# An MoE layer's row gathers, emitted one block further ahead on GpSimd

## The chip, the cores and the metric

The kernel runs on one core of one Trainium2 chip. The metric is the time of one execution on the device, in microseconds. Each number for the whole kernel is the median of three runs.

## The reference

The reference is one decoder layer over 1024 tokens of width 1024, in float32: a mixer (attention heads and RWKV-7 heads), and behind it a mixture of experts. Only the second part is touched here. Each token goes to 6 of 64 experts, and every expert is a SwiGLU with an inner width of 256:

```python
def swiglu(x, wg, wu, wd):
    return (jax.nn.silu(x @ wg) * (x @ wu)) @ wd
...
    def block(args):
        tok, w, e = args
        y = swiglu(h[tok], w_gate[e], w_up[e], w_down[e])
        return y * w[:, None]
...
    x = x + g2 * moe_ffn(h, ...)
return rms_norm(x, final_g)
```

So for each block of assignments the rows of its tokens are gathered, multiplied with three matrices of one expert, weighted, and summed by token. A shared expert does the same for all tokens.

## The kernel before, in words

The mixer and the router take the first 1130 us or so. Then the MoE part runs over a list of blocks (`blocks`, lines 2038 to 2040). Blocks 0 to 7 are the shared expert on 128 tokens each. Blocks 8 to 91 are the routed ones: the experts are ranked by how many tokens they got, an expert has one to four blocks, and a block has 24 to 128 rows. 84 routed blocks belong to 64 experts. What doesn't fit into these blocks would be done in a loop at the end (`rest`).

For a routed block the work is this:

- **Slots** (`slots`, line 1932): an indirect DMA issued by GpSimd reads the list `sl` of the block from `d_slot`, a token number and a weight for each row.
- **Gather** (`rows`, line 1940): an indirect DMA issued by GpSimd reads the token rows from `d_h2` into `xg`, one of 4 buffers of 128 x 1024. The token numbers in `sl` are its indices, so it needs the slots landed.
- **Turn** (`turn`, lines 1952 and 1965): TensorE transposes the rows into `tp`; ScalarE and VectorE write a high and a low part, `xh` and `xl`. These are the transposes that need the gather landed.
- **Up** (`up`, line 1976), **SwiGLU** and **down** (`down`, line 1976 with output `yd`): matmuls in split precision with the parts of the weights.
- **Product** (`result`, line 2026): VectorE multiplies the two halves of `yd` by the row's weight and the gate `g2` into `ye`, one of 3 buffers.
- **Scatter** (`result`, line 2028): an indirect DMA issued by GpSimd adds `ye` to the rows of `d_acc`. All scatters write the same tensor, so each waits until the one before it has landed.

Each expert's weights, 3 MB, are loaded by SyncE (`fetch`, line 1884) a few experts ahead, and split into parts by ScalarE (`guh`, `wdh`) and VectorE (`gul` at line 1898, `wdl` at line 1905).

The order on each engine is the order in which the loop in `experts` emits, and an engine does its instructions in that order. In round `b` of the loop the up matmuls of block `b` are emitted, then the gather of block `b + 3` and the slots of block `b + 5`, then the turn of block `b + 1`, the down matmuls of block `b - 1` and last the product and the scatter of block `b - 1`:

```python
elif b > 6:
    need_x(b + 3)
if b > 7:
    need_s(b + 5)
...
if b > 0:
    result(zs, blocks[b - 1][2], weight_of(b - 1), tis[b - 1])
```

GpSimd thus has, for each round, a gather, a list of slots and a scatter. `need_t` emits no instruction: it takes the column of token numbers out of `sl`. The first five lists of slots are emitted by `dispatch` (line 2085), before the routed blocks. `final` (line 2198) loads `d_acc` once all scatters have landed, and takes the last norm.

Of the kernel before, what the change touches and what calls it, by code (L numbers as in the profile page):

```python
# [8 lines left out]
F32 = mybir.dt.float32  # L9
# [28 lines left out]
class Kern:  # L38
# [1804 lines left out]
    def phase_b(self, pg, close_a4, h2):  # L1843
# [6 lines left out]
        B, sets, wds, xts = {}, [], [], []  # L1850
# [22 lines left out]
        def expert_pools():  # L1873
            close_a4()
            B["wp"] = wp = pool("bw1", 1, side="right")
            sets.append(weight_set(wp))
# [51 lines left out]
            yield [("set", ("shared w", 0))]  # L1928

        def slots(idx, n):  # L1930
            sl = B["fp"].tile([128, 2], F32, name="sl", bufs=8)
            nc.gpsimd.indirect_dma_start(out=sl[0:n], out_offset=None, in_=self.d_slot, in_offset=ind(idx[0:n]))  # L1932
            return sl

        def tokens(sl, n):
            return sl.bitcast(I32)[0:n, 0:1]

        def rows(ti, n):
            x = B["fp"].tile([128, D], F32, name="xg", bufs=4)
            nc.gpsimd.indirect_dma_start(out=x[0:n], out_offset=None, in_=self.d_h2, in_offset=ind(ti), bounds_check=T - 1,  # L1940
                                         oob_is_err=False)
            return x
# [101 lines left out]
        def need_w(k):  # L2044

            for kk, to, which in ((k, raws, GU), (k - 1, rawd, DN)):
                if 0 < kk < NK:
                    to[kk] = fetch(self.eid[0:1, order[kk]:order[kk] + 1], which)

        def need_s(b):  # L2050
            if b < NB:
                k, j, n = blocks[b]
                r = order[k]
                sls[b] = slots(self.sidx[j][:, r:r + 1], n) if r >= 0 else None

        def need_t(b):
            if b < NB:
                tis[b] = tokens(sls[b], blocks[b][2]) if sls[b] else self.toki[:, b:b + 1]

        def need_x(b):  # L2060
            if b < NB:
                k, j, n = blocks[b]
                if k == 0:
                    x = xs[b] = B["fp"].tile([128, D], F32, name="xg", bufs=4)
                    nc.sync.dma_start(x, self.d_ht[j])
                else:
                    xs[b] = rows(tis[b], n)
# [4 lines left out]
        def pieces(n):  # L2072
            for _ in range(n):
                while work and next(work[0], "end") == "end":
                    work.pop(0)

        def dispatch():
            yield [("wait", ("route", 7))]
            expert_pools()
            yield from self.ranks(pg)  # L2080
            for k in range(1, 4):
                need_w(k)
            yield from self.leftover(pg)
            yield [("wait", ("block pools", 0))]
            for b in range(8, 13):
                need_s(b)
                yield [("POOL", 1.0)]
            yield [("DMA", 4.0)]
            yield [("set", ("slots", 0))]

        def experts():

            yield [("wait", ("block pools", 0))]
            yield [("wait", ("shared w", 0))]
            for b in range(8):
                i = blocks[b][1]
                sls[b], tis[b] = None, self.toki[:, i:i + 1]
            xs[0] = h2[6]
            for b in (1, 2):
                need_x(b)  # L2100
            G = ("alloc", ("g", 2)), ("free", "g")
            xt = turn(xs[0], 128)
            yield [("PE", .9), ("ACT", 1.0), ("~DVE", 1.2)]
            act = None
            for b in range(NB + 1):
                if b < NB:
                    k, j, n = blocks[b]
                    m = max(n, MIN_M)
                    two = xt[1] is None
                    for s in up(xt, sets[k % 2], m):  # L2110
                        if b < 8:
                            yield s
                    z = B["z"]
                    if b < 5:
                        yield [("wait", ("T", blocks[b + 3][1]))]
                        need_x(b + 3)
                    elif b == 6:
                        yield [("wait", ("slots", 0))]
                        for i in range(8, 12):
                            need_t(i)  # L2120
                        need_x(8)
                        need_x(9)
                    elif b > 6:
                        need_x(b + 3)
                    if b > 7:
                        need_s(b + 5)
                    turnover = k + 1 < NK + 1 and (blocks[b - 1][0] != k if k else b == 6)
                    if turnover and k + 1 < NK:
                        work.append(split_gu(raws[k + 1], k + 1))
                    pieces(3)  # L2130
                    if turnover and b < 8:
                        yield [("~ACT", 1.7), ("~DVE*", 1.8)]
                if b < NB and two:
                    low(z)
                if act is not None:
                    at = act_t(*act)
                    if b < 8:
                        yield [G[0], ("PE", .25), ("ACT", .3), ("DVE", .35), G[1]]
                if b + 1 < NB:
                    xt = turn(xs[b + 1], blocks[b + 1][2], b < 7)  # L2140
                    if b < 8:
                        yield [("~ACT", 1.0), ("~DVE*", 1.2)]
                if b < NB and two:
                    join(z)
                if act is not None:
                    for s in down(at, act[1]):
                        if b < 8:
                            yield s
                    zs = B["zs"]
                if b < NB:  # L2150
                    act = swiglu(z, m), m
                    pieces(99)
                    if b < 8:
                        yield [("~ACT", .6), ("~DVE", .35)]
                if b > 0:
                    result(zs, blocks[b - 1][2], weight_of(b - 1), tis[b - 1])
                    if b < 8:
                        yield [("~DVE", 1.35), ("~POOL", 1.0)]
                if b < NB:
                    if k and blocks[b - 1][0] != k:  # L2160
                        work.append(split_d(rawd[k]))
                        pieces(99)
                    if b > 7:
                        need_t(b + 4)
                    if turnover:
                        need_w(k + 4)
                    if turnover and b < 8:
                        yield [("~ACT", 2.0), ("~DVE", 2.3), ("~POOL", 1.0)]
# [93 lines left out]
```

## Time and profile before

| | us |
|---|---|
| median of 3 runs (lowest, highest) | 2097.12 (2080.12, 2115.2) |
| profiled execution | 2093.02 |
| its span, first to last instruction | 2091.1 |

| engine, whole span | busy us | share |
|---|---|---|
| TensorE (PE) | 1858.6 | 89% |
| VectorE (DVE) | 1470.3 | 70% |
| ScalarE (ACT) | 933.1 | 45% |
| GpSimd (POOL) | 859.6 | 41% |

A row of a timeline gives an instruction's start, its duration, the engine, the line, the operation and what it writes and reads; in brackets stands how long the engine was idle before it and what ended that. An indirect DMA on POOL is busy there while GpSimd issues it; its data lands later. "Issue" as the end of a wait means that the profile shows nothing that ended it.

### The profile page before, as it was taken

Reading aid. Unit: us, or ns where it says so; the run is one execution under the profiler, and the core shown is the slowest. Engines: PE = TensorE matmul, PEld = TensorE weight load, DVE = VectorE, ACT = ScalarE, POOL = GpSimd, SP = SyncE. Lnnn points to the kernel's source line nnn. Section 1 sums busy time; section 2 is a strip of 40 time slices with the busy share of each in tenths; the row PEclk is TensorE's granted clock in tenths of the full one; section 3 lists DMA queues with packets and bytes.
Section 4 is the critical chain, followed back from the end, with each engine's and each line's share of the span. In section 5 each row is a group of like instructions: output and inputs, shape, how many; then the busy total and the mean of one; then the engine's idle time right before and its main releaser. Section 6 shows DMA issues by size and latency. Waiting matters only on the chain. (4 is left out here: it accounts for less than half of the span.)

```text
span 2091.1 us, 28436 instructions
## 1 busy us (share of the span) xinstructions
PE 1858.6 (89%) x9729; PEld 1399.2 (67%) x9729; DVE 1470.3 (70%) x2561; ACT 933.1 (45%) x1431; POOL 859.6 (41%) x660
## 2 busy tenths in 40 slices
PE   3999999969997997997999799989988989989993
PEld 3777677747876664654787687767756767766771
DVE  7736867939457555656677758878767878878894
ACT  5443433312322332344323236556545656666673
POOL 1201110100012232335455634765656767766662
PEclk7999789969987888998999899999989999999997
DMA  7125345462756648964664589989889999988874
GB/s 270 36 81 126 88 111 129 131 156 71 216 148 183 190 123 237 133 195 137 229 211 147 159 277 322 314 256 318 293 261 309 304 305 307 326 297 297 307 242 174
DMA packets 268579, 440.03 MB, mean 210 GB/s; under 512 B 127445, under 2 KB 197161, under 8 KB 242450
## 3 DMA queue, kind: packets, MB, share of 16 engines
q1 hardware_dynamic: 210978, 365.47, 54.0%
q0 software_dynamic: 26176, 58.91, 12.4%
q10 hardware_dynamic: 31280, 13.83, 2.5%
q8 instruction: 78, 1.28, 0.3%
q14 instruction: 67, 0.55, 0.1%
HBM read 355.27 MB, written 94.90 MB: 215 GB/s over the span
## 5 line engine op out<-in xcount | busy, mean ns | idle before, releaser
L2028 POOL DMA_INDIRECT d_acc<-ye,sl x84 | 192.1, 2287 | 253.4 <-issue 56.2
L1932 POOL DMA_INDIRECT sl<-d_slot,d_sidx x84 | 201.6, 2400 | 27.5 <-issue 24.7
L1904 ACT ACTIVATE wdh<-down 128x1024 fp32r<-128x1024 f32 x128 | 128.7, 1053 | 82.2 <-PE yd L1976 82.2
L1898 DVE TENSOR_TENSOR gul<-up,guh 128x1024 fp32r<-128x1024 f32 x128 | 155.5, 1215 | 10.4 <-ACT guh L1897 9.7
L1940 POOL DMA_INDIRECT xg<-d_h,sl x84 | 149.0, 1774 | 25.6 <-issue 20.7
L1898 DVE TENSOR_TENSOR gul<-gate,guh 128x1024 fp32r<-128x1024 f32 x128 | 155.2, 1213 | 1.7 <-ACT guh L1897 1.7
L1905 DVE TENSOR_TENSOR wdl<-down,wdh 128x1024 fp32r<-128x1024 f32 x128 | 150.1, 1210 | 0.8
L2026 DVE SCALAR_TENSOR_TENSOR ye<-yd,sl,g 128x512 f32<-128x512 f32 (+12 forms) x168 | 120.2, 740 | 32.0 <-PE yd L1976 32.0
L1897 ACT ACTIVATE guh<-gate 128x1024 fp32r<-128x1024 f32 x128 | 134.1, 1047 | 18.8 <-DMA gate<-in_exp_w_gate_dram 18.8
L1976 PE MATMUL yd<-wdh,ah 128*128 128x512 f32 (+6 forms) x368 | 130.5, 438 | 8.5 <-ACT ah L2012 6.7
L1897 ACT ACTIVATE guh<-up 128x1024 fp32r<-128x1024 f32 x128 | 135.1, 1055 | 1.5 <-DMA up<-in_exp_w_up_dram 1.5
L450 PE MATMUL zp<-hTh,whi 128*128 128x512 f32 x480 | 132.4, 414 | 1.4 <-ACT whi L373 1.4
L450 PE MATMUL zp<-hTl,whi 128*128 128x512 f32 x480 | 132.1, 412 | 0.0
L450 PE MATMUL zp<-hTh,wlo 128*128 128x512 f32 x480 | 131.9, 413 | 0.0
L1976 PE MATMUL gu<-guh,xh 128*128 128x512 f32 (+6 forms) x504 | 127.3, 394 | 0.8 <-ACT xh L1959 0.5
L1976 PE MATMUL gu<-guh,xl 128*128 128x512 f32 (+6 forms) x504 | 127.4, 395 | 0.1
L1976 PE MATMUL yd<-wdh,al 128*128 128x512 f32 (+6 forms) x368 | 123.4, 418 | 4.2 <-DVE al L2014 3.7
L1976 PE MATMUL gu<-gul,xh 128*128 128x512 f32 (+6 forms) x504 | 127.0, 394 | 0.0
L1976 PE MATMUL yd<-wdl,ah 128*128 128x512 f32 (+6 forms) x368 | 122.3, 415 | 0.3 <-DVE wdl L1905 0.3
L2012 ACT ACTIVATE ah<-g 128x256 fp32r<-128x256 f32 (+5 forms) x92 | 31.2, 339 | 179.0 <-PE g L2010 178.3
L450 PEld LDWEIGHTS zp<-hTh,whi 128*128 128x128 f32 x480 | 92.6, 198 | 26.4 <-issue 5.5
L1976 PEld LDWEIGHTS gu<-guh,xh 128*128 128x128 f32 (+6 forms) x504 | 89.1, 177 | 29.1 <-ACT xh L1959 1.0
(477 smaller groups left out, 4238.9 us busy)
## 6 DMA issues: line engine op xcount, KB each, us to landing
gate<-in_exp_w_gate_dram SPq DMA_DIRECT2D x64, 1024.0 KB
up<-in_exp_w_up_dram SPq DMA_DIRECT2D x64, 1024.0 KB
down<-in_exp_w_down_dram SPq DMA_DIRECT2D x64, 1024.0 KB
mw<-in_ada_w_dram SPq DMA_DIRECT2D x32, 512.0 KB
wraw<-in_w_in_dram SPq DMA_DIRECT2D x30, 512.0 KB
xw<-in_ada_w_dram SPq DMA_DIRECT2D x8, 1024.0 KB
xw<-in_x_dram SPq DMA_DIRECT2D x8, 512.0 KB
fb<-d_fb SPq DMA_DIRECT2D x16, 256.0 KB
```

Of the source, the lines that this page charges most:

```text
L450: nc.tensor.matmul(z, a[:, d, :], b[:, d, hs], start=(n == 0 and d == 0), stop=(n == 2 and d == 7))
L1897: nc.scalar.activation(gh[:, qs, n, :], t[:, qs], AF.Copy)
L1898: nc.vector.tensor_sub(gl[:, qs, n, :], t[:, qs], gh[:, qs, n, :].bitcast(F32))
L1904: nc.scalar.activation(dh[:, j], raw[0][:, j], AF.Copy)
L1905: nc.vector.tensor_sub(dl[:, j], raw[0][:, j], dh[:, j].bitcast(F32))
L1932: nc.gpsimd.indirect_dma_start(out=sl[0:n], out_offset=None, in_=self.d_slot, in_offset=ind(idx[0:n]))
L1940: nc.gpsimd.indirect_dma_start(out=x[0:n], out_offset=None, in_=self.d_h2, in_offset=ind(ti), bounds_check=T - 1, oob_is_err=False)
L1976: nc.tensor.matmul(z, x[:, d, :], w[:, d, cs], start=(m == 0), stop=(m == 3 * n - 1))
L2012: nc.scalar.activation(ah[:, :, 0:n], tp[:, :, 0:n], AF.Copy)
L2026: nc.vector.scalar_tensor_tensor(y[0:n, hs], zs[h][0:n], wt, B["g2"][0:n, hs], op0=OP.mult, op1=OP.mult)
L2028: nc.gpsimd.indirect_dma_start(out=self.d_acc, out_offset=ind(ti), in_=y[0:n], in_offset=None, bounds_check=T - 1, oob_is_err=False, compu ...
```

## The change

In round `b` the gather is now that of block `b + 4` and the list of slots that of block `b + 6`. Since the emission stands ahead of the scatter of block `b - 1` as before, each gather and each list comes one scatter earlier in GpSimd's order than it did. `dispatch` emits six lists of slots in place of five, and round 7 emits two gathers, those of blocks 10 and 11. The slots get a ninth buffer.

```diff
-            sl = B["fp"].tile([128, 2], F32, name="sl", bufs=8)
+            sl = B["fp"].tile([128, 2], F32, name="sl", bufs=9)
...
-            for b in range(8, 13):
+            for b in range(8, 14):
                 need_s(b)
...
                     elif b == 6:
                         yield [("wait", ("slots", 0))]
-                        for i in range(8, 12):
+                        for i in range(8, 14):
                             need_t(i)
-                        need_x(8)
-                        need_x(9)
+                        for i in range(8, 10):
+                            need_x(i)
                     elif b > 6:
-                        need_x(b + 3)
+                        if b == 7:
+                            need_x(10)
+                        need_x(b + 4)
                     if b > 7:
-                        need_s(b + 5)
+                        need_s(b + 6)
+                        need_t(b + 6)
...
-                    if b > 7:
-                        need_t(b + 4)
```

The first place is on GpSimd, at the end of `dispatch` and the first routed blocks. Numbers tell buffers apart; `sl` are lists of slots, `xg` gathered rows, `ye` products, `toki` the token numbers of a shared block. Before:

```order
L1932 DMA sl_10191<-d_slot_193,d_sidx3_10076 128x2
L1932 DMA sl_10193<-d_slot_193,d_sidx0_10070 128x2
L1940 DMA xg_10195<-d_h2_191,sl_10185 128x1024
L1940 DMA xg_10199<-d_h2_191,sl_10187 128x1024
L2028 DMA d_acc_194<-ye_10237,toki_6875 1152x1024
L1940 DMA xg_10294<-d_h2_191,sl_10189 128x1024
L2028 DMA d_acc_194<-ye_10336,toki_6875 1152x1024
L1940 DMA xg_10367<-d_h2_191,sl_10191 128x1024
L1932 DMA sl_10371<-d_slot_193,d_sidx0_10070 128x2
L2028 DMA d_acc_194<-ye_10419,toki_6875 1152x1024
```

The same place in the changed kernel:

```order
L1932 DMA sl_10193<-d_slot_193,d_sidx0_10070 128x2
L1932 DMA sl_10195<-d_slot_193,d_sidx0_10070 128x2
L1940 DMA xg_10197<-d_h2_191,sl_10185 128x1024
L1940 DMA xg_10201<-d_h2_191,sl_10187 128x1024
L2028 DMA d_acc_194<-ye_10239,toki_6875 1152x1024
L1940 DMA xg_10296<-d_h2_191,sl_10189 128x1024
L1940 DMA xg_10300<-d_h2_191,sl_10191 128x1024
L2028 DMA d_acc_194<-ye_10342,toki_6875 1152x1024
L1940 DMA xg_10373<-d_h2_191,sl_10193 128x1024
L1932 DMA sl_10377<-d_slot_193,d_sidx0_10070 128x2
L2028 DMA d_acc_194<-ye_10425,toki_6875 1152x1024
```

One more list stands ahead of the first gather, and the fourth gather has moved in front of a scatter. From there on each gather is one scatter further ahead.

The second place is on GpSimd, too, in the middle of the routed blocks, around the gather with 108 rows of block 39 (`xg_13179` before, `xg_13072` in the changed kernel) and the scatter of block 34 (`ye_13118` before, `ye_13124` in the changed kernel). Before:

```order
L1940 DMA xg_13066<-d_h2_191,sl_12882 56x1024
L1932 DMA sl_13070<-d_slot_193,d_sidx0_10070 96x2
L2028 DMA d_acc_194<-ye_13118,sl_12430 1152x1024
L1940 DMA xg_13179<-d_h2_191,sl_12957 108x1024
L1932 DMA sl_13183<-d_slot_193,d_sidx0_10070 96x2
L2028 DMA d_acc_194<-ye_13231,sl_12543 1152x1024
```

And in the changed kernel:

```order
L2028 DMA d_acc_194<-ye_13011,sl_12248 1152x1024
L1940 DMA xg_13072<-d_h2_191,sl_12888 108x1024
L1932 DMA sl_13076<-d_slot_193,d_sidx0_10070 96x2
L2028 DMA d_acc_194<-ye_13124,sl_12361 1152x1024
L1940 DMA xg_13185<-d_h2_191,sl_12963 96x1024
L1932 DMA sl_13189<-d_slot_193,d_sidx0_10070 128x2
```

The gather of 108 rows stood behind the scatter of block 34 and now stands in front of it, where the gather of 56 rows stood. The lists of slots have moved with the gathers, so between a block's list and its gather there are as many instructions as before.

## Rows read from the trace of the kernel before

**Rows 1.** The page: TensorE's granted clock in 40 slices of the span, tenths.

```profile
PEclk7999789969987888998999899999989999999997
```

**Rows 2.** Waits of PE from 1200 us on: total us, times, longest.

```profile
PE tp L1965 <- DMA xg<-d_h,sl: 39.1, 11, 9.8
PE tp L1952 <- DMA xg<-d_h,sl: 6.4, 2, 5.7
```

**Rows 3.** Timeline of POOL, 1499 to 1540 us.

```profile
1500.05 6.08 POOL L1940 DMA_INDIRECT xg<-d_h,sl  x1 [0.31 <-issue]
...
1509.52 7.16 POOL L2028 DMA_INDIRECT d_acc<-ye,sl  x1 [2.15 <-DVE ye L2026]
1516.98 1.52 POOL L1940 DMA_INDIRECT xg<-d_h,sl  x1 [0.30 <-issue]
...
1528.19 1.60 POOL L2028 DMA_INDIRECT d_acc<-ye,sl  x1 [6.24 <-issue]
```

**Rows 4.** Timeline of PE, 1519 to 1534 us.

```profile
1521.22 0.39 PE L2010 MATMUL g<-idf,act 128*128 128x128 f32 x2
1531.45 1.68 PE L1965 MATMUL tp<-idf,xg 108*128 108x108 f32 x8 [9.84 <-DMA xg<-d_h,sl]
```

**Rows 5.** Timeline of DVE, 1497 to 1520 us.

```profile
1499.49 2.35 DVE L1905 TENSOR_TENSOR wdl<-down,wdh 128x1024 fp32r<-128x1024 f32 x2
...
1504.03 1.22 DVE L1898 TENSOR_TENSOR gul<-gate,guh 128x1024 fp32r<-128x1024 f32 x1
...
1508.11 1.40 DVE L2026 SCALAR_TENSOR_TENSOR ye<-yd,sl,g 108x512 f32<-108x512 f32 x2
```

**Rows 6.** The tile xg: durations in ns (min/median/max), first and last start; landing.

```profile
L1965 PE MATMUL tp<-idf,xg x440: 229/276/451, 1206.0 to 2005.2; 128*128 128x128 f32 x80, 96*128 96x96 f32 x21, 72*128 72x72 f32 x12, 120*128 120x120 f32 x11
...
L1940 POOL DMA_INDIRECT xg<-d_h,sl x84: 942/1102/6232, 1193.6 to 2027.1; - x84
...
DMA to landing us min/median/max: 4.3/10.3/14.4
```

**Rows 7.** Line 2028, the scatters: durations in ns, first and last start.

```profile
L2028 POOL DMA_INDIRECT d_acc<-ye,sl x84: 1362/1608/7284, 1236.7 to 2059.3; - x84
```

**Rows 8.** Busy time of each engine in the routed stage, 1206 to 2058 us.

```profile
1206.00:2058.00 852.00, 796.10 (x3689) 605.05 (x3688) 686.46 (x890) 508.72 (x748) 536.50 (x245) 0.96 0.88 289
```

**Rows 9.** Busy times, then granted clock; ten stretches, one shown, and their sum.

```profile
1531.40:1538.20 6.80, 6.75 (x20) 5.11 (x21) 2.29 (x4) 4.28 (x6) 3.12 (x3) 0.50 0.41 91
...
sum 49.10, PE 49.02 PEld 36.69 DVE 26.85 ACT 24.09 POOL 22.52; mean PE 4.90 PEld 3.67 DVE 2.68 ACT 2.41 POOL 2.25
```

**Rows 10.** Timeline, 1500 to 1550 us: two down matmuls at either clock.

```profile
1515.03 0.62 PE L1976 MATMUL yd<-wdl,ah 128*108 128x512 f32 x2
...
1534.70 1.05 PE L1976 MATMUL yd<-wdl,ah 128*128 128x512 f32 x2
```

**Rows 11.** DMA issues, 1206 to 2060 us: median us from issue to landing.

```profile
d_acc<-ye,sl POOLq DMA_INDIRECT x84, 8.8
```

**Rows 12.** Timeline of POOL: scatters at both ends of a stretch, and near the end.

```profile
1638.65 1.49 POOL L2028 DMA_INDIRECT d_acc<-ye,sl  x1 [2.85 <-DVE act L2004]
...
1697.86 7.28 POOL L2028 DMA_INDIRECT d_acc<-ye,sl  x1 [4.45 <-DVE ye L2026]
...
1969.49 2.15 POOL L2028 DMA_INDIRECT d_acc<-ye,sl  x1 [3.25 <-DVE wdl L1905]
```

**Rows 13.** Timeline of DVE, 1630 to 1690 us: the first and last product.

```profile
1631.28 1.40 DVE L2026 SCALAR_TENSOR_TENSOR ye<-yd,sl,g 96x512 f32<-96x512 f32 x2
...
1685.07 0.75 DVE L2026 SCALAR_TENSOR_TENSOR ye<-yd,sl,g 128x512 f32<-128x512 f32 x1 [0.43 <-PE yd L1976]
```

**Rows 14.** Waits of SP, 1206 to 2060 us.

```profile
SPq L1884 <- DVE gul L1898: 388.1, 76, 27.7
```

**Rows 15.** Waits of DVE, 1206 to 2058 us.

```profile
DVE ye L2026 <- PE yd L1976: 31.7, 48, 2.0
```

**Rows 16.** Groups of POOL, 1206 to 2060 us: busy us, mean ns, idle before.

```profile
L2028 POOL DMA_INDIRECT d_acc<-ye,sl x84 | 192.1, 2287 | 253.4 <-issue 56.2 <-DVE gul L1898 43.1 <-DVE ye L2026 38.0
```

## The prediction

> **What bounds the kernel now.** The page first: TensorE is granted close to full clock over the second half of the span, with dips [rows 1]. Those dips and the idle time lie in one place, the stage of 84 routed blocks from about 1206 us on. The view of waits, for TensorE in that stage, names one large cause: the transposes of a block's token rows wait for the gather xg, 39.1 us in 11 waits and 6.4 us in 2, the longest 9.8 us [rows 2]. So 45.5 us are lost to late gathers.
>
> Why are they late? The timeline of GpSimd shows its order, gather, slots, scatter, and the next gather only behind the scatter [rows 3]. The scatter of one block adds into the same accumulator as the one before and waits until that one has landed. One chain: the scatter started at 1509.52 runs 7.16 us; the gather behind it starts at 1516.98; TensorE, which needs those rows from 1521.6 on, gets them at 1531.45, after a wait of 9.84 us [rows 3, 4]. Counted back from the last, the product that VectorE finished at 1508.11 + 1.40 = 1509.51 [rows 5] is scattered only at 1528.19, 18.7 us later, after 6.24 us in which GpSimd waited for the landing before it. GpSimd is thus behind, and its long instructions have a visible neighbour: the gather at 1500.05 starts inside VectorE's splits wdl and gul, which run from 1499.49 to 1504.03 + 1.22 = 1505.25 without a pause; it takes 6.08 us and ends 0.88 us after them [rows 3, 5].
>
> The Trainium skill, "SBUF — State Buffer", section "SBUF: two separate sides", has a rule for this, which speaks against the change: VectorE and GpSimd share a port pair under an exclusive lock, so a DMA issued from GpSimd can't have its descriptors written while VectorE runs an SBUF-to-SBUF operation in a two-port mode. The trace agrees for starts that fall into a split (6.08 and 7.16 us against medians of 1.10 and 1.61 [rows 3, 6, 7]). By it the sum below would be some 5 us worse, an estimate: VectorE's density would rise from 686.46 of 852 us to 686.46 of 787 [rows 8], 8% more, on about 10 held scatters of 5.6 us each. I don't count this.
>
> **What the change does, part by part.** No instruction is added or removed; on TensorE, VectorE, ScalarE and SyncE the order is the same. On GpSimd every gather and every list of slots moves three instructions forward, past one adding scatter. The gather that waited behind the scatter of 1509.52 would stand where another stands now, at 1500.05: it ends at 1506.13 and lands at the latest 1500.05 + 14.4 = 1514.5 [rows 6], 7 us before TensorE asks at 1521.6. In general the lead grows by one block. The 84 scatters start from 1236.7 to 2059.3, 822.6 / 83 = 9.91 us apart [rows 7]; the longest wait is 9.84 us. Taken singly, every one of the 13 waits is covered: 45.5 us.
>
> The clock comes on top. Ten stretches, of which one stands with the sum, eight of which follow such a wait, hold 49.1 us at a granted 0.5, the 1.2 GHz level, with TensorE busy for 49.0 of them [rows 9]. Two matmuls take 1.05 us there and 0.62 us at the full clock [rows 10]: 1 - 0.62 / 1.05 = 0.41, times 49 is 20 us. Together 65 us is the most that can go.
>
> What comes back is GpSimd's own pace, since the waits are also what lets it catch up. Without waits TensorE would take (822.6 - 65) / 83 = 9.13 us a block. GpSimd's chain from scatter to scatter is bounded from below by the median landing, 8.8 us [rows 11], and the shortest gap between its instructions, 0.3 us [rows 3]: 9.1 us, so nothing comes back. It is bounded from above by a stretch without a TensorE wait: six steps of the scatters from 1638.65 to 1697.86, 9.87 us each, while the products went from 1631.28 to 1685.07, 8.97 us each [rows 12, 13]. At 9.87 us the 83 steps cost 819 us: 3 us saved, and once the longer lead, about 9 us, so 12. I take 9.5 us, the middle, because the pace differs by kind of block: near the end, with narrower blocks, eleven steps from 1969.49 to 2059.26 take 8.16 us each [rows 7, 12]. Then (9.5 - 9.13) x 83 = 31 us come back, and 65 - 31 = 34 us are gained.
>
> Smaller parts. One more list of slots stands before the first gather: at about a gather's median run and the gap, 1.1 + 0.3 us; the first gather starts at 1193.6, lands 10.3 us later (median) at 1203.9 and is needed at 1206.0 [rows 6], so 2.1 us hide it; without that cover it would cost 1.4 us once, and it can't gain. The ninth slot buffer keeps the distance between a buffer's old and new list in scatters: nothing. A gather's own buffer is free before its turn: it stands behind a scatter whose product TensorE makes after the transposes that empty the buffer. So no wait is added there; if one were, the slots and the scatter behind the gather would wait too. Weights: SyncE's loads wait for VectorE to empty their buffers, 388.1 us under gul alone [rows 14], so they have lead and aren't next at 9.13 us a block. If that were wrong, ScalarE would wait for gate or down.
>
> What is late next is the ring of three product buffers, ye. VectorE now never waits for it: its waits at ye are all for TensorE, 31.7 us [rows 15]. But the scatter of 1528.19 began 18.7 us after its product; with 8.8 us to land that makes 27.5 us, and three blocks of 9.13 us are 27.4 us. With gathers out of the way the backlog can grow to that wall, and VectorE then waits in front of ye, with wdl and gul queued behind it and TensorE behind those. This is where I expect the 31 us that come back.
>
> **The sum.** The profiled execution took 2093.0 us, 1.9 us of it outside its span of 2091.1, and lies 4.1 us under the median of the three runs, 2097.1. 2093.0 - 34 = 2059 for an execution like it; against the median, 2097.1 - 34 = 2063 us. A measurement of this kernel can tell a difference of about 2%, 42 us.
>
> **The rivals.**
> - All of it goes: GpSimd holds 9.1 us. For it: the narrow blocks at 8.16 us, and the waits are single spikes after a held scatter. Against: the six steps of 9.87 us. 2097.1 - 65 = 2032 us.
> - GpSimd sets the pace: 9.87 us a block, only the lead is gained, and VectorE's wait for ye takes the place of TensorE's for xg. For it: GpSimd runs behind almost all the time, and only 38.0 us of its 253.4 us before scatters end with a product [rows 16]. 2097.1 - 12 = 2085 us.
> - Slower, by a backlog at the ye wall: a product that has waited for a landing is followed at once by wdl and gul, and the next scatter starts into them and takes 7.2 us instead of 1.6, so it lands 5.6 us later, and the next product waits again. In the trace the excess of the mean over the median scatter, (2287 - 1608) ns x 84 = 57 us, is about 10 such [rows 7, 16]. It eats the 34 us from 34 / 5.6 = 6 further held scatters on, and is 2% slower from (34 + 42) / 5.6 = 14. With 12 more: 12 x 5.6 = 67 us, 2063 + 67 = 2130 us. Against it: a stall of VectorE also opens a gap for GpSimd.
> - It doesn't do what it says: the moved gather waits for its slots. Four GpSimd instructions still stand between the two, and the gaps before gathers are 0.3 us now [rows 3]. 2097 us.
>
> **How the numbers follow.** Part of it comes back 0.50 (2063, its own range 2045 to 2080); all goes 0.20; GpSimd's pace 0.20; slower 0.08; not as said 0.02. Two per cent faster is under 2055: all of the second case and three tenths of the first, 0.35. Over 2139 is slower by 2%: half of the slower case, 0.04. The rest is 0.61. The range reaches from 2032, the full gain, to 2092, past the case of GpSimd's pace.
>
> **What would show it.** Right: TensorE's waits for xg under 15 us in all; its clock dips mostly gone; VectorE's waits at ye with a d_acc landing as releaser, 10 to 40 us, where there are none now; the scatters 9.4 to 9.6 us apart. Wrong on the sum, if ye shows no such waits (all goes), or if the scatters stay at 9.9 us (GpSimd's pace). Wrong on the mechanism, if xg still holds TensorE for over 30 us, or if the mean scatter grows past 3 us.

## The result and the profile after

The changed kernel takes 2112.18 us (median of 20 runs, 2094.08 to 2128.14), the kernel before, run beside it, 2095.01 us (20 runs, 2077.02 to 2115.2). The ratio is 1.006, with a 95% interval of 1.0034 to 1.0086: a little slower, where 2063 us and a range up to 2092 were forecast. The profiled execution has a span of 2110.8 us against 2091.1.

The waits of TensorE in the routed stage, from 1200 us on (total us, times, longest):

```profile
PE tp L1965 <- DMA xg<-d_h,sl: 28.7, 10, 5.2
PE yd L1976 <- DVE al L2014: 18.9, 24, 2.9
PE tp L1952 <- DMA xg<-d_h,sl: 9.9, 4, 4.0
```

The waits for late gathers have shrunk from 45.5 us [rows 2] to 28.7 + 9.9 = 38.6 us, and no single one is longer than 5.2 us. A row that was 3.7 us has grown to 18.9 us: TensorE waits for VectorE.

The waits of VectorE in the same stretch:

```profile
DVE ye L2026 <- DMA d_acc<-ye,sl: 39.6, 14, 8.8
DVE ye L2026 <- issue: 37.4, 9, 8.8
DVE ye L2026 <- PE yd L1976: 20.5, 24, 2.7
```

The first two are new: the kernel before had only the third kind [rows 15]. A product `ye` waits until the scatter that reads its old buffer has landed. This is called a stop at the ring below, the ring being the three buffers of `ye`. The "issue" row is taken for the same wait where the profile doesn't show the landing: its longest is the same 8.8 us, and behind 21 of the 23 stops of both rows the next scatter, which waits for a landing too, starts 0.68 to 0.77 us after the product. Together the two rows are 77.0 us.

The scatters' line (duration in ns min/median/max, first and last start):

```profile
L2028 POOL DMA_INDIRECT d_acc<-ye,sl x84: 1322/1610/7887, 1239.3 to 2079.0; - x84
```

The chain of scatters runs from 1239.3 to 2079.0, 839.7 / 83 = 10.12 us a step, against 9.91 [rows 7]. That is 839.7 - 822.6 = 17.1 us; the first scatter starts 2.6 us later; the sum is 19.7 us, the whole difference of the two spans (2110.8 - 2091.1).

What a step is made of can be read where the trace holds a scatter's landing (42 of the 84 before, 43 after). On average it lands 6.5 us after the end of its issue, before and after, and the next scatter starts 1.1 us after that, before and after. With the mean issue a step is 2.29 + 6.5 + 1.1 = 9.9 us before and 2.60 + 6.5 + 1.1 = 10.2 us after. The earlier gathers thus don't slow the landings. Counted from the start of the issue their median is 8.3 us, against 8.8 [rows 11], their mean 8.9 against 8.8:

```profile
d_acc<-ye,sl POOLq DMA_INDIRECT x84, 8.3
```

What has grown is the issue. The groups of POOL on the page (busy us, mean ns | idle before):

```profile
L2028 POOL DMA_INDIRECT d_acc<-ye,sl x84 | 218.1, 2596 | 249.7 <-issue 65.8
...
L1940 POOL DMA_INDIRECT xg<-d_h,sl x84 | 177.9, 2118 | 25.8 <-issue 19.7
L1932 POOL DMA_INDIRECT sl<-d_slot,d_sidx x84 | 168.7, 2009 | 27.6 <-issue 24.4
```

The median scatter is unchanged (1610 ns, before 1608), the mean has gone from 2287 [rows 16] to 2596 ns: (2596 - 2287) x 84 = 26 us more in long scatters. Gathers are longer too (1774 before), lists shorter (2400 before).

The whole routed stage, 1206 to 2079 us (busy times of PE, PEld, DVE, ACT and POOL, then granted clock, DMA share, GB/s):

```profile
1206.00:2079.00 873.00, 804.29 (x3694) 606.81 (x3692) 684.56 (x891) 508.87 (x748) 557.29 (x245) 0.96 0.87 282
```

POOL is busy for 21 us more (557.29 against 536.50 [rows 8]) and TensorE for 8 (804.29 against 796.10); VectorE does as much as before in more time, and the mean clock is the same 0.96. The dips of the clock haven't gone: there are eleven stretches at half clock up to the last scatter. One of them stands here, with the sum of the first ten; the eleventh holds 3.4 us:

```profile
1525.60:1532.40 6.80, 6.50 (x19) 4.96 (x20) 3.14 (x6) 4.28 (x6) 4.75 (x3) 0.50 0.62 168
...
sum 64.90, PE 55.79 PEld 39.95 DVE 43.44 ACT 30.09 POOL 42.88; mean PE 5.58 PEld 4.00 DVE 4.34 ACT 3.01 POOL 4.29
```

TensorE is busy for 55.8 + 3.4 = 59.2 us at the 1.2 GHz level, against 49.0 [rows 9].

How the new wait works is seen at the place of [rows 3 to 5]. POOL first:

```profile
1489.45 7.37 POOL L2028 DMA_INDIRECT d_acc<-ye,sl  x1 [0.30 <-issue]
...
1507.15 7.79 POOL L2028 DMA_INDIRECT d_acc<-ye,sl  x1 [7.47 <-DVE ye L2026]
...
1523.96 4.39 POOL L2028 DMA_INDIRECT d_acc<-ye,sl  x1 [5.92 <-DVE ye L2026]
...
1536.39 1.64 POOL L2028 DMA_INDIRECT d_acc<-ye,sl  x1 [5.43 <-DVE ye L2026]
```

And VectorE:

```profile
1506.38 1.41 DVE L2026 SCALAR_TENSOR_TENSOR ye<-yd,sl,g 108x512 f32<-108x512 f32 x2 [7.52 <-DMA d_acc<-ye,sl]
1507.71 2.35 DVE L1905 TENSOR_TENSOR wdl<-down,wdh 128x1024 fp32r<-128x1024 f32 x2
...
1512.24 1.22 DVE L1898 TENSOR_TENSOR gul<-gate,guh 128x1024 fp32r<-128x1024 f32 x1
...
1523.19 1.41 DVE L2026 SCALAR_TENSOR_TENSOR ye<-yd,sl,g 108x512 f32<-108x512 f32 x2 [7.38 <-issue]
```

One landing, that of the scatter of 1489.45, ends both waits: VectorE's for its buffer at 1506.38 and GpSimd's for its accumulator at 1507.15. The two then start side by side (the scatter starts before the product made there is finished, at 1506.38 + 1.41 = 1507.79, so it reads an older one). VectorE goes straight from the product into wdl and gul, and the scatter takes 7.79 us instead of 1.6. The next product is stopped again at the next landing (1523.19), and the next scatter runs 4.39 us; the one after that isn't held (1.64 us). It isn't so at every stop: of the 22 scatters that start within 1.4 us of a stopped product 6 run over 3 us, and their mean is 2.97 us against 2.46 of the other 62. "DVE ye" as releaser of the scatter is thus only an event close by in time, and the landing is what it waited for.

TensorE feels both brakes here (timeline of PE):

```profile
1507.95 1.10 PE L1952 MATMUL tp<-idf,xg 56*128 56x56 f32 x8 [3.63 <-DMA xg<-d_h,sl]
...
1513.81 1.19 PE L1976 MATMUL yd<-wdh,al 128*108 128x512 f32 x2 [2.79 <-DVE al L2014]
```

So even a gather issued one block earlier comes late: GpSimd has fallen that much further behind.

### The profile page after: what moved, and what is told of

Its sections match the earlier page's. It is cut to its first block, busy times and chain, and to the rows that moved or that the text cites. A ratio compares the mean times of both kernels' runs of the same rounds, so it can differ in the third digit from the quotient of the medians.

```text
span 2110.8 us, 28436 instructions
## 1 busy us (share of the span) xinstructions
PE 1859.1 (88%) x9729; PEld 1397.0 (66%) x9729; DVE 1468.1 (70%) x2561; ACT 933.3 (44%) x1431; POOL 883.1 (42%) x660
## 5 line engine op out<-in xcount | busy, mean ns | idle before, releaser
L2028 POOL DMA_INDIRECT d_acc<-ye,sl x84 | 218.1, 2596 | 249.7 <-issue 65.8
L1940 POOL DMA_INDIRECT xg<-d_h,sl x84 | 177.9, 2118 | 25.8 <-issue 19.7
L1932 POOL DMA_INDIRECT sl<-d_slot,d_sidx x84 | 168.7, 2009 | 27.6 <-issue 24.4
L1976 PE MATMUL yd<-wdh,al 128*128 128x512 f32 (+6 forms) x368 | 125.7, 424 | 19.7 <-DVE al L2014 18.9
```

The source lines that it names most:

```text
L1976: nc.tensor.matmul(z, x[:, d, :], w[:, d, cs], start=(m == 0), stop=(m == 3 * n - 1))
L2028: nc.gpsimd.indirect_dma_start(out=self.d_acc, out_offset=ind(ti), in_=y[0:n], in_offset=None, bounds_check=T - 1, oob_is_err=False, compu ...
```

## The experiments

All ratios are to the kernel before, run on the same chip in the same series; in brackets the 95% interval.

### Does the chain of scatters set the pace?

**Two accumulators, order before.**

```diff
-            nc.gpsimd.indirect_dma_start(out=self.d_acc, out_offset=ind(ti), in_=y[0:n], in_offset=None,
+            self.turns += 1
+            to = self.d_acc2 if self.turns % 2 else self.d_acc
+            nc.gpsimd.indirect_dma_start(out=to, out_offset=ind(ti), in_=y[0:n], in_offset=None,
...
```

> The kernel before, with every second scatter added into a second accumulator, so that a scatter waits for the landing of the one two before it. The second accumulator is neither cleared nor added at the end: this part of the sum is left out. Theory W (the wait of each scatter for the one before makes GpSimd's backlog): TensorE's waits for xg fall from 45.5 us to under 10, the scatters come 9.1 to 9.3 us apart, 2035 to 2050 us against some 2095. Theory H (the backlog comes from GpSimd's starts being held by VectorE's splits): the waits for xg stay over 25 us, 2080 to 2100 us.

Measured: 2038.93 us, 0.9702 [0.9637, 0.9768]. TensorE's waits for xg (total us, times, longest), then the scatters' line:

```profile
PE tp L1967 <- DMA xg<-d_h,sl: 3.0, 4, 1.2
...
PE tp L1954 <- DMA xg<-d_h,sl: 0.3, 1, 0.3
```

```profile
L2032 POOL DMA_INDIRECT d_acc<-ye,sl x84: 1362/1655/6884, 1237.2 to 2007.0; - x84
```

With gathers where they were, the 45.5 us of waits have shrunk to 3.3 us, and the step is (2007.0 - 1237.2) / 83 = 9.27 us. The late gathers were a symptom: a scatter's wait for the landing before it made them late. The dips of the clock went with them but for one of 3.4 us at the end. From 1206 to 2001 us the mean granted clock (the third number from the end) is full, against 0.96 [rows 8]:

```profile
1206.00:2001.00 795.00, 779.67 (x3708) 594.62 (x3706) 682.45 (x891) 507.44 (x748) 599.89 (x247) 1.00 0.94 314
```

**Two accumulators, changed order** (the same edit).

> The changed kernel with the same second accumulator, left out of the sum in the same way. Theory W: without the backlog the ring of ye never fills, VectorE's waits at ye for landings fall from some 80 us to under 10, and the time is that of the first run within 10 us. Theory C (gathers issued earlier take bandwidth from the scatters, whatever waits for what): it stays 15 us or more slower than the first run.

Measured: 2039.86 us, 0.9717 [0.9652, 0.9782], no wait for xg, 0.6 us of VectorE at the ring. Without the chain the change is worth nothing in either direction. Theory C, contention of the earlier gathers with the scatters as a cost of its own, has fallen; a slower landing could hide where no scatter waits for it, but with one accumulator the landings didn't slow either (6.5 us after the issue in both kernels).

**Two accumulators, whole computation, order before**: the second accumulator is cleared by nine writes and added at the end.

```diff
+            for i in range(SLOTS // 128):
+                nc.sync.dma_start(self.d_acc2[i * 128:(i + 1) * 128, :], z)
...
+                x2 = fp.tile([128, D], F32, name=f"w{i}")
+                nc.scalar.dma_start(x2, self.d_acc2[i * 128:(i + 1) * 128, :])
+                nc.vector.tensor_add(x, x, x2)
```

> The kernel before with two accumulators, the second cleared beforehand by nine writes of 0.5 MB and loaded and added at the end. By the first run's 2039 us, and 4 MB more to load at the end at the rate at which the first 4 MB come (some 10 us), plus up to 10 us for the clearing: 2045 to 2062 us, faster than both kernels.

Measured: 2051.91 us, 0.9757 [0.9693, 0.9822]. It is faster than both kernels; clearing and adding give back 0.9757 - 0.9702 = 0.55%, some 12 us, of what the first run gained (most likely; the two intervals overlap).

### What do VectorE's splits do to it?

**Low parts left out, order before, and changed order.**

```diff
-                    nc.vector.tensor_sub(gl[:, qs, n, :], t[:, qs], gh[:, qs, n, :].bitcast(F32))
+                    if k < 4:
+                        nc.vector.tensor_sub(gl[:, qs, n, :], t[:, qs], gh[:, qs, n, :].bitcast(F32))
...
-                nc.vector.tensor_sub(dl[:, j], raw[0][:, j], dh[:, j].bitcast(F32))
+                self.nsplit = getattr(self, "nsplit", 0) + 1
+                if self.nsplit < 9:
+                    nc.vector.tensor_sub(dl[:, j], raw[0][:, j], dh[:, j].bitcast(F32))
```

> The kernel before without most of VectorE's splits: the low parts gul and wdl are made for the first experts alone and are stale after that; the matmuls run as before. Theory S (a start of GpSimd's that falls into a split is held, and holds are what stretches the chain from scatter to scatter): no scatter runs over 3.5 us, the chain is landing and issue alone, 6.6 + 1.6 + 0.7 = 8.9 us, waits for xg fall under 15 us, 2025 to 2050 us. Theory L (the landing alone sets the chain): waits for xg stay over 30 us, 2075 to 2100 us.

> The changed kernel without most of VectorE's splits, as in the run before. Theory S: with nothing to be held by, the loss goes too: VectorE waits for ye landings under 15 us, and the time is within 8 us of the run before. Theory L: it stays 10 us or more slower than the run before, with ye waits over 50 us.

Measured: 2052.62 us, 0.9752 [0.9691, 0.9814], with the order before; 2052.65 us, 0.976 [0.9702, 0.9818], with the changed one. VectorE's waits in the changed order, then its scatters:

```profile
DVE ye L2029 <- issue: 49.3, 20, 4.6
DVE ye L2029 <- DMA d_acc<-ye,sl: 48.9, 19, 4.6
```

```profile
L2031 POOL DMA_INDIRECT d_acc<-ye,sl x84: 1321/1520/1660, 1253.8 to 2022.4; - x84
```

No scatter runs longer than 1.66 us (2.09 with the order before). VectorE is stopped at the ring for 49.3 + 48.9 = 98 us, more than in the changed kernel, and yet the change costs nothing. So the ring's stops alone cost nothing; it takes the splits as well for the change to cost.

Not all that was expected came. With the order before 23.1 us of waits for xg are left where Theory S gave under 15, and the time lies 3 us above its range; and Theory S gave under 15 us of stops at the ring, not 98. The edit also does two things at once: it takes away what holds the scatters, and it lowers VectorE's busy time from 686 to 297 us of the 852, so that VectorE has time to make up for a stop. These runs can't tell the two apart. The sum of a step in the section on the result speaks for the first: what grew there is the scatters' issue.

### Is it the ring of products?

**Four products, order before** (xg gives up a buffer), **and changed order** (down gives up a raw buffer).

```diff
-            x = B["fp"].tile([128, D], F32, name="xg", bufs=4)
+            x = B["fp"].tile([128, D], F32, name="xg", bufs=3)
...
-            y = B["fp"].tile([128, D], F32, name="ye", bufs=3)
+            y = B["fp"].tile([128, D], F32, name="ye", bufs=4)
```

```diff
-                t = B["wp"].tile([128, j, c], F32, name=n, bufs=3)
+                t = B["wp"].tile([128, j, c], F32, name=n, bufs=2 if n == "down" else 3)
...
-            y = B["fp"].tile([128, D], F32, name="ye", bufs=3)
+            y = B["fp"].tile([128, D], F32, name="ye", bufs=4)
```

> The kernel before with three buffers of xg in place of four and four of ye in place of three. Its gathers look three blocks ahead, so three buffers hold them. Both theories: VectorE doesn't wait for ye landings in the kernel before, so a fourth buffer gives nothing: 2085 to 2105 us, waits for xg 35 to 55 us.

> The changed kernel with four buffers of ye; for the room, the raw down weights have two buffers in place of three. Theory R (the ring of three ye buffers is what turned the lead into a loss, by VectorE's stop in front of it): VectorE's waits at ye fall from some 80 us to under 35, TensorE's for xg stay under 40, 2060 to 2095 us. Theory P (GpSimd's pace alone sets the time): the backlog fills the fourth buffer too, the waits at ye stay over 60 us, 2105 to 2120 us.

Measured: 2100.24 us, 0.9975 [0.9938, 1.0013], and 2130.35 us, 1.014 [1.0067, 1.0212]. In the second VectorE no longer stops at the ring, as Theory R had it, but the time lies above the ranges of both theories, and the waits for gathers are back (PE, total us, times, longest):

```profile
PE tp L1965 <- DMA xg<-d_h,sl: 56.9, 20, 8.2
PE tp L1952 <- DMA xg<-d_h,sl: 6.9, 5, 2.3
```

At first this looked as if a longer ring made it worse. It had a second edit in it, the down buffer, and so three controls were run.

**Changed order with two down buffers; order before with two; order before with two and four products** (single lines of the diffs above).

> The changed order, with the raw buffers of the down weights at two in place of three and nothing else: the control for the run with four products, which had to give up that buffer. If the buffer costs nothing, the ratio is that of the change, 1.004 to 1.009, and the 1.014 of the run with four products was the longer ring's own. If the buffer is what cost there, the ratio is 1.012 to 1.018, ScalarE or VectorE wait longer for the loads of down, and the run with four products says only that a longer ring gains nothing.

> The kernel before with the raw buffers of the down weights at two and nothing else: the control for the two runs that had it with the changed order (1.0243 with three products, 1.014 with four). Theory K (the changed order costs by VectorE's stop at the ring of products, which ends on the same landing as GpSimd's wait for its scatter, so that splits and scatter start together): the buffer by itself costs 0.8 to 1.8%, ratio 1.008 to 1.018, and with four products the changed order comes out level with this run. Theory L (the buffer costs only together with the changed order): the ratio is 0.997 to 1.005, and the changed order loses about 1% even where the ring never stops VectorE.

> The kernel before with two raw buffers for down and four products: the fourth corner of the square of order and ring. Theory K: the order before never reaches the ring, so the fourth buffer changes nothing, and this run stands within 0.4% of the one with three products (both orders then cost the same where the ring is long). Theory L: the same level, but 1% under the changed order with four products.

Measured, with the mean scatter of the page and the step from first to last scatter start:

| two down buffers | ratio | mean scatter ns | step us |
|---|---|---|---|
| before, 3 products | 1.0113 [1.0079, 1.0146] | 2383 | 10.20 |
| before, 4 products | 1.0121 [1.007, 1.0172] | 2407 | 10.18 |
| changed, 4 products | 1.014 [1.0067, 1.0212] | 2381 | 10.20 |
| changed, 3 products | 1.0243 [1.0199, 1.0287] | 2607 | 10.54 |

The ratios come from three series, each to the kernel before of its own. A step is of one execution each, in the first row the longest of its ten (2129.92 us, median 2114.72). The down buffer costs 1.1% by itself, and the three kernels in which the ring never stops VectorE agree within their intervals. Only the fourth stands out, by 1.0 to 1.3% and above what was expected of it in either case (its interval lies clear of those of the two with the order before, and just touches that of the wider third, which is of four executions). Its VectorE waits:

```profile
DVE ye L2026 <- DMA d_acc<-ye,sl: 58.0, 19, 7.9
DVE ye L2026 <- issue: 40.0, 8, 9.3
```

And its scatters on the page:

```profile
L2028 POOL DMA_INDIRECT d_acc<-ye,sl x84 | 219.0, 2607 | 306.1 <-issue 81.7
```

So it isn't the place of the gathers in the order by itself that costs: with a ring long enough the change is level as far as these intervals tell, though no gain. What fits is that it costs through VectorE's stops at the ring. Of the 0.34 us a step more, 0.22 us are longer scatters.

**Two products, order before, and changed order.**

```diff
-            y = B["fp"].tile([128, D], F32, name="ye", bufs=3)
+            y = B["fp"].tile([128, D], F32, name="ye", bufs=2)
```

> The kernel before with two buffers of ye in place of three; the gathers stand where they stood. Theory B (it matters which engine the backlog stops: VectorE in front of ye, with its splits right behind, costs more than TensorE in front of xg): VectorE waits for ye landings over 60 us, TensorE's waits for xg fall under 30, more scatters are held than 11, 2110 to 2150 us. Theory O (the gathers' place in GpSimd's order is what costs, by what it does to the queue): 2085 to 2110 us, held scatters 9 to 13.

> The changed order, with the ring of products ye at two buffers in place of three. Theory D (the change costs because GpSimd falls further behind, so that more scatters start inside VectorE's splits and are held; a shorter ring stops VectorE one block earlier and cuts the backlog back to that of the kernel before): the ratio falls from 1.006 to 0.998 to 1.003, as the kernel before had with two buffers (1.003), the mean scatter falls from 2596 ns to under 2400, and TensorE's waits for xg fall under 25 us. Theory G (the order itself costs, a gather standing in front of the scatter it used to follow): the ratio stays at 1.006 or above and scatters stay 10.1 us apart. Theory R2 (every wait of VectorE for the ring is lost time): two buffers double those waits, 77 us in the changed kernel, and the ratio goes past 1.015.

Measured: 2102.55 us, 1.0028 [0.9983, 1.0072], and 2134.28 us, 1.0187 [1.0144, 1.023]. The second has no wait for xg left, and instead (VectorE):

```profile
DVE ye L2026 <- DMA d_acc<-ye,sl: 126.9, 38, 11.0
```

```profile
L2028 POOL DMA_INDIRECT d_acc<-ye,sl x84 | 228.2, 2717 | 268.5 <-issue 85.9
```

TensorE waits for VectorE in place of gathers:

```profile
PE yd L1976 <- DVE al L2014: 49.2, 32, 3.2
```

Theory D, that a shorter ring would help by keeping GpSimd closer, has fallen; its rival, that the ring's stops cost, got the size right. This is the forecast's aim reached in full, TensorE never waiting for a gather, at a price of 1.9%. Of 37 scatters that start beside a stopped product 13 run over 3 us, of the other 47 only 4.

The first of the two is a miss the other way. VectorE's stops and TensorE's waits for xg (26.0 us) came as Theory B had them, but the time is in the range of Theory O. VectorE's waits:

```profile
DVE ye L2026 <- DMA d_acc<-ye,sl: 45.5, 13, 7.3
DVE ye L2026 <- issue: 24.2, 9, 8.9
```

These 69.7 us of stops at the ring under the order before cost 0.3% at the most likely, with a mean scatter of 2406 ns. They were read from the shortest of this kernel's ten executions (2087.6 us), so a usual execution may have more. The stops don't have one fixed price, and that the order adds something of its own where the ring is short isn't ruled out.

### Gathers or slots?

**Slots alone, in the order before; gathers alone** (the second against the changed kernel).

```diff
-            sl = B["fp"].tile([128, 2], F32, name="sl", bufs=8)
+            sl = B["fp"].tile([128, 2], F32, name="sl", bufs=9)
...
-            for b in range(8, 13):
+            for b in range(8, 14):
...
-                        need_s(b + 5)
+                        need_s(b + 6)
```

```diff
-            sl = B["fp"].tile([128, 2], F32, name="sl", bufs=9)
+            sl = B["fp"].tile([128, 2], F32, name="sl", bufs=8)
...
-            for b in range(8, 14):
+            for b in range(8, 13):
...
-                        need_s(b + 6)
-                        need_t(b + 6)
+                        need_s(b + 5)
+                        need_t(b + 5)
```

> The kernel before, with the lists of slots alone one block further ahead (nine buffers, six lists in dispatch) and the gathers where they were. All theories expect nothing: a ratio of 0.997 to 1.003, TensorE's waits for xg 35 to 55 us, scatters 9.8 to 10.0 us apart. If the slots are what costs, 1.004 or above.

> The kernel before, with the gathers alone one block further ahead and the lists of slots where they were. Theory D and theory G: the gathers carry the whole change, so a ratio of 1.003 to 1.010, VectorE's waits for a landing in front of ye 50 to 90 us, scatters 10.0 to 10.25 us apart. If the shorter distance from a list to its gather matters (a gather that waits for its list holds the scatter behind it), 1.010 to 1.03 with waits of GpSimd in front of the gathers that a list's landing ends.

Measured: 2098.88 us, 1.0021 [0.9982, 1.006], for the slots: nothing that can be told. And 2130.36 us, 1.0173 [1.0131, 1.0215], for the gathers, whose group on the page has a new releaser:

```profile
L1940 POOL DMA_INDIRECT xg<-d_h,sl x84 | 164.5, 1959 | 194.3 <-DMA sl<-d_slot,d_sidx 84.2
```

GpSimd now stands 194.3 us in front of gathers instead of 25.8, 84.2 of them put down to the list's landing, and the scatter queued behind a gather stands with it. (72.4 more are put down to TensorE's transposes; the changed kernel, which differs by the lists alone, has 0.9 of these.) Moving the slots too was thus the needed part of the change: the gathers carry the cost, and the slots keep it from being larger.

### What slows the landing?

**No weight loads after the third expert, order before, and changed order.**

```diff
+            old = B.setdefault("old", {}).setdefault(which[0][0], [])
+            if len(old) >= 3:
+                old.append(old[-3])
+                return old[-1]
```

> The kernel before, with the routed experts' weights loaded for the first three experts alone and used again from their buffers by all others (the results of the others are not theirs); splits, matmuls, gathers and scatters as before. If the 290 GB/s of weight loads slow the landing of the scatters, the landing falls from a median of 8.8 us to under 7 and the pace to 9.3 us or less, ratio 0.95 to 0.98, with few waits for xg. If the landing is the scatter's own, it stays at 8 to 9 us and the ratio is 0.99 to 1.0.

> The changed order, with the same loads left out (weights of the first three experts used by all). If the loads slow the landings, it equals the run of the kernel before without loads within 0.4%, since the ring then stops VectorE for under 20 us. If the landing is the scatter's own, the change costs here what it costs with the loads, 0.4 to 0.9% over the kernel before without loads.

Measured: 2031.25 us, 0.9701 [0.9645, 0.9757], and 2029.29 us, 0.9705 [0.965, 0.976]. The issues of the first in the routed stage (median us to landing), then its scatters' line:

```profile
d_acc<-ye,sl POOLq DMA_INDIRECT x84, 6.3
```

```profile
L2033 POOL DMA_INDIRECT d_acc<-ye,sl x84: 1362/2002/6884, 1230.9 to 1998.1; - x84
```

The landing falls from 8.8 [rows 11] to 6.3 us, and the step to (1998.1 - 1230.9) / 83 = 9.24 us. Both orders give one time. So about a quarter of the landing that makes up the chain is owed to the weight loads that run beside it. The step is that of two accumulators (9.27 us) and no wait of TensorE for a gather is left: the chain no longer sets the pace here either.

## Why the prediction was wrong

**What held.** The late gathers exist, the longest of them follow scatters that were held, and the change does cover those (9.8 us before, 5.2 after). The rival "doesn't do what it says" is out, as are the small parts: the ninth slot buffer and the extra list cost nothing (the run with the slots alone). The ring of three products is what was late next, as the prediction named it, with waits of 77 us where 10 to 40 were given; but what came of it was more than the 31 us it was to bring back. By the prediction's own signs its mechanism was wrong: xg still holds TensorE for 38.6 us, over the 30 it named, and the scatters are further apart than in either of its cases.

**The step that failed** is the choice of GpSimd's pace: "I take 9.5 us, the middle", out of 9.1 to 9.87 us. It measured 10.12 us, above both ends. At 9.5 us a block 31 us came back of 65; at 10.12 us all 65 come back and 17 us more. The upper end was a stretch of the kernel before with next to no wait of TensorE (one of 0.5 us), taken as GpSimd's worst. At the lower end the term that was mis-sized is the gap: 0.3 us is the shortest gap between any two instructions of GpSimd, but from a landing to the next scatter's start it is 1.10 us on average, and with the mean landing of 8.84 us that is 9.94 us, the step of the kernel before. The step isn't a constant of GpSimd either. It is a scatter, its landing and the next start, and the two-accumulator runs show that this loop, not TensorE, set the pace of the stage in the kernel before: 9.91 us with it, 9.27 without. Where a loop on another engine sets the pace, TensorE's idle time is the amount by which that loop is slower, and moving gathers within the loop's engine doesn't shorten the loop. The 65 us were not on offer to this change. Two accumulators took most or all of them: 66 us between the medians of that series (2104.61 - 2038.93), 52 us between the profiled executions (2091.1 - 2038.8).

**The clue that was there.** The prediction weighed 9.1 us, median landing plus gap, as a lower bound for a chain that "holds", and gave the rival "GpSimd sets the pace" 0.20. The row on idle time before scatters spoke for that rival (38.0 of 253.4 us ended by a product [rows 16]), and the average step of 9.91 us was already GpSimd's own. A sum of the loop's parts that comes out under its measured step has left something out, here 0.8 us of the gap.

**The slower rival's mechanism** happened, at a smaller size. It said that a product which waited for a landing is followed at once by wdl and gul, and that the next scatter starts into them. The timeline at 1506 us shows it twice in a row, and 6 of 22 scatters beside a stopped product were held. Its price was 5.6 us for each further held scatter, and 2% from 14 of them on; the excess measured is 26 us, as much as 4.6 of them. Its assumed baseline of 34 us gained was not there, so that much was enough to end 0.6% slower. The four-run square, at the edge of what its intervals can tell, and the run with two products (1.9%) say that the ring's stops carry this cost, and the pair without low parts that it takes the splits as well.

**The rule on the shared port.** In the traces, a scatter is long only where VectorE's splits run: without low parts none exceeds 1.66 us in the changed order. The prediction put this down to a rule of the Trainium skill, "SBUF — State Buffer", section "SBUF: two separate sides": an exclusive lock between VectorE and GpSimd, which a VectorE operation in a two-port mode takes. By the same section of the Trainium skill (its part "Who interferes with whom") the splits aren't such operations: tensor_tensor, which they are (TENSOR_TENSOR in the rows), has no two-port mode, contends with GpSimd only where GpSimd reads, and wasn't seen to stall a DMA. Here the DMAs do stall beside them, 7.79 us instead of 1.6 at 1507 us, and for this case the measurement decides. Which port or lock holds them, no run here shows. The prediction sized the effect by VectorE's density, which was to rise by 8%. It fell, from 686.46 / 852 = 81% [rows 8] to 684.56 / 873 = 78%, while the mean scatter grew by 309 ns. Density thus didn't size it; the scatters beside stopped products (2.97 us against 2.46) point to when the splits start.

**The clock** followed the waits and gave nothing back: eleven dips in place of ten, at other places. Where the waits went, with two accumulators in the order before, the dips went too but for one.

**What stays open.** The share of held scatters among the ring's costs is read from single executions (0.22 of 0.34 us a step in the square; 0.31 us of longer scatters against 0.21 us a step between the two kernels), so other parts move too, and a scatter that starts beside a stopped product isn't the only one that grows: between the two kernels the 22 beside a stop hold some 15 of the 26 us more, 22 x (2.97 - 2.29). Why 70 us of stops cost 0.3% in the order before with two products, and 77 us cost 0.6% with the changed order, wasn't settled. Nor was why two down buffers cost 1.1%.

## What to carry to other kernels

Before moving an instruction to cover a wait, find the loop that sets the pace: divide the stage by its blocks for each engine, and ask of the slowest what one turn is made of; a wait on another engine is then only the difference. A chain of adding scatters into one tensor is such a loop, of issue, landing and restart, and here it was shortened by breaking the chain (two accumulators: 2.4% with clearing and adding), not by reordering around it. More lead for one queue let a backlog grow until the next ring was full, and what ran right behind that ring's stop seems to have mattered.

## What the runs showed of the hardware

- A scatter's landing depends on what else is loaded: a median of 8.8 us beside 289 GB/s of traffic [rows 8, 11], 6.3 us without the weight loads, beside 69 GB/s.
- A GpSimd DMA was long only where it met VectorE's splits. From 1200 us on, 51 of its indirect DMAs before and 64 after ran over 1 us longer than usual (1.6 us for a scatter, 1.0 for a gather or a list); every one overlapped a split, and with the low parts left out there was none. With two accumulators the mean scatter was 2726 ns and with no loads 2823 ns, longer than in the changed kernel's 2596, and these kernels are 3% faster: a long issue costs only where the chain is the limit.
- A third raw buffer for down is worth 1.1% of this kernel, though without it ScalarE, which reads it first, has no wait for a load of down; the scatters' step grows (10.20 us against 9.91) and TensorE's wait for gathers with it (72.9 us against 45.5).
